# The beginning of a two-layer decoder kernel is rearranged: loads, splits, fillers, and the place of sums and maxima

## Chip, core and metric

One Trainium2 chip, one of its cores. The metric is the device time of one execution in microseconds (us); lower is better. Three runs of the kernel before gave 600.25, 600.36 and 603.13 us, with a median of 600.36 us.

## What is computed

Two layers over 256 tokens of width 1024, all in float32: an mLSTM mixer and a convolutional feed-forward, then block attention and a second feed-forward. Only the first steps of the mixer matter here:

```
u = rmsnorm(x, norm_g) @ w_in
q, k, v, o, gi, gf = split(u)            # 512, 512, 1024, 1024, 4, 4 columns
i_pre, f_pre = gi + b_gates[0], gf + b_gates[1]
lf   = log_sigmoid(f_pre);  bcum = cumsum(lf)          # over time
m_t  = running maximum over time of (i_pre - bcum)     # stabiliser
s    = (q k^T) * exp(decay built from bcum, i_pre, m_t)
h    = (s @ v) / max(|sum s|, exp(-m_t))
```

The norm needs one mean of squares per token; the kernel multiplies with unnormalised x (times the gain) and scales the products by that token's reciprocal root afterwards.

## The kernel before

Every float32 product is made from two parts. `split` (L176) and `unit` (L164) round an operand to a `hi` part on ScalarE (ACT) and leave the rest as `lo` on VectorE (DVE, `lo = raw - hi`); TensorE (PE) then runs hi times (hi, lo) as one 512-column matmul and lo times hi as one of 256 columns (`steps_w`, L227) or three of 512 columns (`steps_x`, L254). A weight unit is 128 x 2048 floats (1 MB): one DMA into one of three `raw` buffers, two halves on ACT, two on DVE into one of four `hi`/`lo` buffer pairs. A new load can go out only when DVE has read the buffer's last content, and a new `hi` can be made only when PE has finished with the buffer's last content.

PE's order is the order of the program (a manual schedule); `mix` (L69) runs a list of costed steps and calls other items when the running cost reaches the number written beside them. The orders of the other engines come from a scheduler when the kernel is built. So a place in PE's order is fixed by those numbers, and what stands ahead of an instruction on DVE or ACT must be read from the built program.

The beginning runs so. SP issues, in one queue, x (`hT`, 8 blocks of 128 rows), the gate weights and gains (`fst`), the first unit of `w_kq` in four pieces and the second in two, with the small broadcast `row` between those two (L103 to L117). PE runs eight warm-up matmuls (L129). x is split into `xa` by block (L181, L182). PE then runs eight steps k of three products each: the gates (L503) and the first two columns j = 0 and 1 of the eight k/q columns, five matmuls a step; then columns j = 2 to 7, eight steps of two matmuls each. Beside that:

- squares of x on GpSimd (POOL, L398), their running sum `sqacc` on DVE (L400);
- `r.sums` (L213) reads `sqacc` on PE, in column j = 2 after six of its steps; `ms` on DVE and `rc` on POOL (L217) follow;
- `gates` (L431) and `r.row` (L222) need `rc`; the columns j = 0 to 2 are read out of PSUM and scaled once `r.row` is there (L490), the others after that;
- `sums_f` (L444) and `maxima` (L453), late in the columns; `maxima` starts a chain of nine small DVE operations (L454, L458) that ends in `mh` (ACT) and `ml` (DVE) at L178 and L179;
- `tab` and `gcol` (L606 to L615), needed only in the second layer, on POOL.

Then come the v and o products (`block_x`, four blocks of two units of `w_vo`, sixteen steps of three 512-column matmuls). In the second of them stand the four `decay` items (L474, L475), which read `mh` and `ml`; after them `floors` and `scores`.

Of the kernel before, what the change touches and what calls it, by code (L numbers as in the profile page):

```python
# [18 lines left out]
P = 128  # L19
D = 1024  # L20
S = 256
# [18 lines left out]
WARM = 8  # L40
# [41 lines left out]
def yoco_kernel(ctx: ExitStack, tc: tile.TileContext, A, out):  # L82
# [41 lines left out]
    nc.scalar.activation(const.tile([P, 1], F32, name="tables"), mhalf[:, :1], AF.Exp)  # L124
    warm = const.tile([P, 512], BF16, name="warm")
    nc.vector.memset(warm, 0.0)
    for j in range(WARM):
        ps = pmis.tile([P, 512], F32, name="mis")
        nc.tensor.matmul(ps, warm[:, :P], warm, start=True, stop=True)  # L129
    nc.gpsimd.memset(wgs.bitcast(F32), 0.0)  # L130


    ident = const.tile([P, P], F32, name="ident")
    make_identity(nc, ident)

    both8 = const.tile([P, 2 * MH], F32, name="both8")
    nc.gpsimd.tensor_tensor(out=both8, in0=ident[:, :2 * MH], in1=ident[:, 2 * MH:4 * MH], op=OP.add)

    sel = const.tile([P, MH, P], F32, name="sel")
    nc.gpsimd.memset(sel, 0.0)  # L140
    nc.gpsimd.affine_select(out=sel, in_=sel, pattern=[[-1, MH], [0, P]],
                            compare_op=OP.not_equal, fill=1.0, base=0, channel_multiplier=1)

    tri = const.tile([P, S], F32, name="tri")
    nc.gpsimd.memset(tri, 1.0)
    nc.gpsimd.affine_select(out=tri[:, :P], in_=tri[:, :P], pattern=[[1, P]],
                            compare_op=OP.is_ge, fill=0.0, base=0, channel_multiplier=-1)

    cmask = const.tile([P, S], F32, name="cmask")
    nc.gpsimd.memset(cmask, 0.0)  # L150
    nc.gpsimd.affine_select(out=cmask[:, :P], in_=cmask[:, :P], pattern=[[1, P]],
# [649 lines left out]
```

## Time and profile before

| | |
|---|---|
| median of three runs | 600.36 us |
| profiled execution | 600.34 us, its span 598.6 us |
| PE busy / DVE / ACT / POOL | 590.3 / 494.1 / 392.7 / 172.3 us |
| PE first matmul of the gates, of the columns | 4.77 us, 7.36 us |
| PE at the sums (L213) | 20.90 us |
| PE at the first block of v and o | 37.80 us |
| PE at the first decay (L474) | 50.76 us |

Times count from the span's start. A matmul's row gives its own duration; since matmuls are pipelined, the pace is read from one start to the next.

### The profile page before, as it was taken

What the parts mean: (1) busy time and instruction counts of PE and PEld (TensorE: products, weight loads), DVE (VectorE), ACT (ScalarE), POOL (GpSimd) and SP (SyncE); (2) the same over time, 40 slices, a digit from 0 to 9 for tenths busy, and PEclk for the clock granted to TensorE, in tenths of its full rate; (3) what the DMA queues carried; (4) which work ended last, traced back from release to release, by engine and by line L of the source; (5) the groups of instructions that cost most, each with busy time, mean ns of one, the idle gap of its engine ahead of it and who ended that gap; (6) DMA issues with size and microseconds to landing.
All of it is one profiled execution on the core that took longest, in us unless ns stands there. A gap on an engine that the chain in (4) does not pass through costs nothing.

```text
span 598.6 us, 8993 instructions
## 1 busy us (share of the span) xinstructions
PE 590.3 (99%) x3278; PEld 506.2 (85%) x3278; DVE 494.1 (83%) x837; ACT 392.7 (66%) x713; POOL 172.3 (29%) x188
## 2 busy tenths in 40 slices
PE   7999999999999999999999999999999999999997
PEld 4888888888888888888888888888888888888887
DVE  5997678979999999987768687467999999998650
ACT  6656776577886767765656687554878767676430
POOL 6500300352545344301111210022546453432000
PEclk9999999999999999999999999999999999999999
DMA  7875334627445543486745533335363456336730
GB/s 249 305 275 178 141 140 142 211 79 273 153 172 175 206 156 115 166 263 215 240 183 211 194 123 125 126 140 209 123 225 146 165 187 211 105 138 208 266 111 19
DMA packets 18621, 105.79 MB, mean 177 GB/s; under 512 B 2320, under 2 KB 3856, under 8 KB 9104
## 3 DMA queue, kind: packets, MB, share of 16 engines
q1 hardware_dynamic: 18576, 105.21, 50.2%
q8 instruction: 26, 0.43, 0.3%
q14 instruction: 19, 0.16, 0.1%
HBM read 104.15 MB, written 1.05 MB: 176 GB/s over the span
## 4 chain that ended last, share of the span: by engine, by line
PE 87%; DVE 6%; ACT 3%; issue 1%; DMA 1%; POOL 1%; SPq 0%; DVEq 0%
PE acc L242 41%; PE acc L246 21%; PE acc L263 6%; PE acc L265 6%; PE acc L264 6%; DVE lo L173 3%; ACT hi L172 1%; DVE xs L349 1%; DVE xa L182 1%; DMA hT<-xT 1%; PE acc L240 1%; PE mis L554 1%; DVE hT L292 1%; PE mis L669 1%; PE acc L681 1%
## 5 line engine op out<-in xcount | busy, mean ns | idle before, releaser
L173 DVE TENSOR_TENSOR lo<-raw,hi 128x1024 fp32r<-128x1024 f32 (+2 forms) x218 | 248.5, 1169 | 29.4 <-ACT hi L172 29.3
L242 PE MATMUL acc<-xb,hi 128*128 128x512 f32 x736 | 252.3, 396 | 0.6 <-POOL xb L352 0.6
L172 ACT ACTIVATE hi<-raw 128x1024 fp32r<-128x1024 f32 (+2 forms) x218 | 199.8, 964 | 55.1 <-PE acc L242 28.8
L246 PE MATMUL acc<-xb,lo 128*128 128x256 f32 x736 | 191.2, 279 | 0.0
L242 PEld LDWEIGHTS acc<-xb,hi 128*128 128x128 f32 x736 | 131.8, 188 | 26.3 <-POOL xb L352 1.3
L246 PEld LDWEIGHTS acc<-xb,lo 128*128 128x128 f32 x736 | 138.7, 188 | 8.0
L242 PE MATMUL acc<-f,hi 128*128 128x512 f32 x330 | 115.0, 394 | 0.0
L330 DVE SCALAR_TENSOR_TENSOR y<-whole,par,y 128x254 f32<-128x254 f32 (+1 forms) x176 | 110.3, 646 | 3.1 <-ACT y L327 2.8
L246 PE MATMUL acc<-f,lo 128*128 128x256 f32 x352 | 96.8, 282 | 0.0
L339 POOL TENSOR_TENSOR a<-sg,y 128x256 f32<-128x256 f32 x44 | 58.7, 1334 | 97.6 <-ACT sg L337 97.6
L242 PEld LDWEIGHTS acc<-f,hi 128*128 128x128 f32 x330 | 61.1, 188 | 13.0
L246 PEld LDWEIGHTS acc<-f,lo 128*128 128x128 f32 x352 | 66.1, 188 | 1.3
L327 ACT ACTIVATE y<-whole,par 128x256 f32<-128x256 f32 x88 | 51.7, 595 | 20.8 <-DVE whole L283 18.8
L242 PE MATMUL acc<-xa,hi 128*128 128x512 f32 x160 | 58.3, 407 | 2.3 <-ACT hi L172 1.8
L263 PE MATMUL acc<-hi,xa 128*128 128x512 f32 x128 | 53.0, 414 | 0.0
L341 POOL TENSOR_TENSOR f<-a,f 128x256 fp32r<-128x256 f32 x44 | 42.3, 962 | 36.3 <-ACT f L340 36.3
L265 PE MATMUL acc<-hi,xa 128*128 128x512 f32 x128 | 50.1, 392 | 0.0
L264 PE MATMUL acc<-lo,xa 128*128 128x512 f32 x128 | 50.0, 391 | 0.0
L200 POOL TENSOR_TENSOR sqacc<-sqacc,sq 128x256 f32<-128x256 f32 x18 | 16.3, 907 | 115.3 <-ACT sq L199 115.3
L246 PE MATMUL acc<-xa,lo 128*128 128x256 f32 x160 | 44.8, 292 | 0.0
L282 ACT ACTIVATE whole<-acc 128x256 f32<-128x256 f32 x97 | 35.4, 368 | 7.7 <-PE acc L242 6.2
L283 DVE TENSOR_TENSOR whole<-acc,whole 128x256 f32<-128x256 f32 x97 | 39.4, 412 | 0.0
(183 smaller groups left out, 637.5 us busy)
## 6 DMA issues: line engine op xcount, KB each, us to landing
raw<-w_up SPq DMA_DIRECT2D x44, 1024.0 KB, 4.8
raw<-w_down SPq DMA_DIRECT2D x32, 704.0 KB, 4.3
raw<-w_kqv SPq DMA_DIRECT2D x12, 1024.0 KB, 4.8
raw<-w_vo SPq DMA_DIRECT2D x8, 1024.0 KB, 4.8
raw<-w_out SPq DMA_DIRECT2D x4, 1024.0 KB, 4.8
raw<-w_o SPq DMA_DIRECT2D x4, 1024.0 KB, 4.8
raw<-w_kq SPq DMA_DIRECT2D x2, 1024.0 KB, 7.6
raw<-w_kq SPq DMA_DIRECT2D x4, 256.0 KB, 5.7
```

Source lines behind the costliest of these rows:

```text
L172: nc.scalar.activation(hi[:, c], raw[:, c], AF.Copy)
L173: nc.vector.tensor_tensor(lo[:, c], raw[:, c], hi[:, c].bitcast(F32), OP.subtract)
L242: nc.tensor.matmul(p, hi[:, c], both[k], start=k == 0, stop=last)
L246: nc.tensor.matmul(p[:, :S], lo[:, c], xh[k], start=False, stop=False)
L263: nc.tensor.matmul(p, xh[k][:, ts], hi[:, c], start=k == 0, stop=False)
L264: nc.tensor.matmul(p, xh[k][:, ts], lo[:, c], start=False, stop=False)
L265: nc.tensor.matmul(p, xl[k][:, ts], hi[:, c], start=False, stop=k == KD - 1)
L283: nc.vector.tensor_tensor(y, ps[:, :S], y, OP.add)
L327: nc.scalar.activation(y, u, AF.Identity, bias=b, scale=w[2])
L330: nc.vector.scalar_tensor_tensor(y[:, d:], u[:, :S - d], w[j], y[:, d:], op0=OP.mult, op1=OP.add)
L339: nc.gpsimd.tensor_tensor(out=a, in0=sg, in1=y[0], op=OP.mult)
L341: nc.gpsimd.tensor_tensor(out=al[i], in0=a, in1=ah[i].bitcast(F32), op=OP.subtract)
```

## The change

It does seven things.

1. The loads of x go out on SP first; the first two pieces (256 KB each) of the first weight unit go out on ACT's queue, the other two on SP behind x; `row` is loaded behind the second unit.
2. The first two weight units are split by hand in a fixed order on ACT and DVE: block by block with x, in pieces of 256, 256, 512, 512, 512 and then 512, 512, 1024 columns, ahead of the squares.
3. The squares move from POOL to ACT (Square), their sums stay on DVE.
4. Ten warm-up matmuls instead of eight, and two fillers of the same kind behind the first step.
5. k and q columns are read out of PSUM into `kq` unscaled and are scaled in place at the end of the columns; no column's read-out waits for `r.row`.
6. `r.sums` moves from cost 1.5 to 6.6, `gates` and `r.row` from 3.2 to 9.5, and `sums_f` and `maxima` from the columns (9.6, 14.0) into the first block of v (1.5, 4.5). Within a step the gates' matmul comes last.
7. The constants are made behind all this in the program, the zeroing of `wgs` moves from POOL to DVE, and `gcol` and `tab` are kept where they stand in the program, behind the mixer.

```diff
-WARM = 8
+WARM = 10
+FILL = 2
...
     nc.sync.dma_start(hT[:, 0], A["xT"][:, 0])
     nc.sync.dma_start(fst, A["first"])
     nc.sync.dma_start(hT[:, 1], A["xT"][:, 1])
+    for j in range(3):
+        k = slice(2 * j + 2, 2 * j + 4)
+        nc.sync.dma_start(hT[:, k], A["xT"][:, k])
     for j in range(4):
         c = slice(j * 512, (j + 1) * 512)
-        nc.sync.dma_start(raw0[:, c], A["w_kq"][0, :, c])
-        if j < 3:
-            k = slice(2 * j + 2, 2 * j + 4)
-            nc.sync.dma_start(hT[:, k], A["xT"][:, k])
+        (nc.scalar if j < 2 else nc.sync).dma_start(raw0[:, c], A["w_kq"][0, :, c])
...
-        if j == 0:
-            nc.sync.dma_start(row, A["row"].to_broadcast([P, N_ROW]))
...
+    warm_up(WARM)
+    nc.vector.memset(wgs.bitcast(F32), 0.0)
...
+    first = ExitStack()
+    first.enter_context(tc.manual_schedule(engines={mybir.EngineType.Activation, mybir.EngineType.DVE}))
+    w0 = [wsp.tile([P, 2048], F32R, name=nm) for nm in ("hi", "lo")]
+    w1 = [wsp.tile([P, 2048], F32R, name=nm) for nm in ("hi", "lo")]
+
+    def piece(w, raw, a, b):
+        split(w[0][:, a:b], w[1][:, a:b], raw[:, a:b])
+
     for k in range(KD):
         split(setA[0][k], setA[1][k], hT[:, k], fst[:, C_ANORM + k:C_ANORM + k + 1])
+        if k < 2 or k % 2 == 1:
+            piece(w0, raw0, (k if k < 2 else k - 1) * 256, (k + 1) * 256)
+        if k == 0:
...
+    for a, b in ((0, 512), (512, 1024), (1024, 2048)):
+        piece(w1, raw1, a, b)
     for k in range(KD):
-        sq = work.tile([P, S], F32, name="sq") if k > 0 else sqacc
-        nc.gpsimd.tensor_tensor(out=sq, in0=hT[:, k], in1=hT[:, k], op=OP.mult)
-        if k > 0:
-            nc.vector.tensor_tensor(sqacc, sqacc, sq, OP.add)
+        squares(k, nc.vector)
+    first.close()
...
-        def kq_done(j):
-            nc.vector.tensor_tensor(kq[j], whole(pk[j]()), r.rB, OP.mult)
...
-                           (lambda p: kq_done(j)) if j > 2 else None)
+                           lambda p: whole(p, kq[j]))
+        def scale(j):
+            nc.vector.tensor_tensor(kq[j], kq[j], r.rB, OP.mult)
...
-        mix([s for k in range(KD) for s in (sg[k], s0[k], s1[k])])
+        for k in range(KD):
+            mix((s0[k], s1[k], sg[k]))
+            if k == 0:
+                warm_up(FILL)
         mix(kq_steps(2)[:1])
+        nc.sync.dma_start(row, A["row"].to_broadcast([P, N_ROW]))
         nc.sync.dma_start(par, A["par"])
         mix(kq_steps(2)[1:] + [s for j in range(3, 8) for s in kq_steps(j)],
-            [(1.5, r.sums), (3.2, gates), (3.2, row_done), (9.6, sums_f), (14.0, maxima)])
+            [(6.6, r.sums), (9.5, gates), (9.5, r.row)])
+        for j in range(2 * MH):
+            scale(j)
...
-        mix(block_x(A["w_vo"], 0, setA, v_done(0)))
+        mix(block_x(A["w_vo"], 0, setA, v_done(0)), [(1.5, sums_f), (4.5, maxima)])
...
-    nc.gpsimd.tensor_copy(gcol, par[:, C_KG:C_KG + 2])
+    tc.keep_in_program_order(nc.gpsimd.tensor_copy(gcol, par[:, C_KG:C_KG + 2]))
```

Where a DVE or ACT instruction lands in the built program is seen in the two orders. First DVE, around the last additions into the sum of squares. Names end in a buffer's number: `raw_94` is the second unit of `w_kq`, `raw_375` or `raw_360` the third, `raw_431` or `raw_428` the fourth, `raw_502` the first unit of `w_vo`, and `ms` is the instruction behind PE's sums. Before, from the second unit's last half on:

```order
L173 TENSOR_TENSOR lo_298<-raw_94,hi_297 128x1024
L283 TENSOR_TENSOR whole_290<-acc_214,whole_290 128x256
L283 TENSOR_TENSOR whole_351<-acc_253,whole_351 128x256
L400 TENSOR_TENSOR sqacc_167<-sqacc_167,sq_202 128x256
L283 TENSOR_TENSOR whole_355<-acc_256,whole_355 128x256
L400 TENSOR_TENSOR sqacc_167<-sqacc_167,sq_205 128x256
L173 TENSOR_TENSOR lo_378<-raw_375,hi_377 128x1024
L215 TENSOR_SCALAR ms_320<-mis_317 128x2
```

In the changed kernel, the last twelve rows up to `ms`; ahead of them stand the same half of the second unit, three additions and three read-outs:

```order
L172 TENSOR_TENSOR sqacc_141<-sqacc_141,sq_189 128x256
L145 TENSOR_TENSOR lo_363<-raw_360,hi_362 128x1024 x2
L172 TENSOR_TENSOR sqacc_141<-sqacc_141,sq_192 128x256
L256 TENSOR_TENSOR kq2_261<-acc_320,kq2_261 128x256
L172 TENSOR_TENSOR sqacc_141<-sqacc_141,sq_195 128x256
L145 TENSOR_TENSOR lo_431<-raw_428,hi_430 128x1024 x2
L256 TENSOR_TENSOR kq3_262<-acc_341,kq3_262 128x256
L172 TENSOR_TENSOR sqacc_141<-sqacc_141,sq_198 128x256
L145 TENSOR_TENSOR lo_505<-raw_502,hi_504 128x1024
L172 TENSOR_TENSOR sqacc_141<-sqacc_141,sq_201 128x256
L145 TENSOR_TENSOR lo_505<-raw_502,hi_504 128x1024
L187 TENSOR_SCALAR ms_384<-mis_381 128x2
```

So the last addition, which PE's sums wait for, now stands behind both halves of the third and of the fourth unit and the first half of the fifth.

Second DVE again, around `ml`, which the second matmul of each decay reads (`V11` is the last v read-out of the first block; `raw_757` and `raw_764` are the sixth unit of `w_vo`, whose `hi` needs the buffer that the first block's last step frees). Before:

```order
L173 TENSOR_TENSOR lo_712<-raw_709,hi_711 128x1024 x2
L179 TENSOR_TENSOR ml_225<-mx0_220,mh_224 4x256
L540 SCALAR_TENSOR_TENSOR V11_506<-acc_558,rc_322,V10_505 128x2x256
L173 TENSOR_TENSOR lo_760<-raw_757,hi_759 128x1024
L477 SCALAR_TENSOR_TENSOR E0_230<-mis_604,av_218,cmask_137 128x256
```

In the changed kernel:

```order
L475 TENSOR_TENSOR mx0_246<-mx1_247 4x256
L559 SCALAR_TENSOR_TENSOR V11_493<-acc_565,rc_386,V10_492 128x2x256
L145 TENSOR_TENSOR lo_767<-raw_764,hi_766 128x1024 x2
L151 TENSOR_TENSOR ml_251<-mx0_246,mh_250 4x256
L494 SCALAR_TENSOR_TENSOR E0_255<-mis_611,av_244,cmask_220 128x256
```

`ml` has moved behind the read-out and behind both halves of the sixth unit. On ACT the same holds of `mh`, which the first matmul of each decay reads. Before:

```order
L172 ACTIVATE hi_711<-raw_709 128x1024 x2
L178 ACTIVATE mh_224<-mx0_220 4x256
L539 ACTIVATE V10_505<-acc_558,rc_322 128x2x256
L172 ACTIVATE hi_759<-raw_757 128x1024 x2
L481 ACT_TABLE_LOAD
```

In the changed kernel:

```order
L144 ACTIVATE hi_718<-raw_716 128x1024 x2
L558 ACTIVATE V10_492<-acc_565,rc_386 128x2x256
L144 ACTIVATE hi_766<-raw_764 128x1024 x2
L150 ACTIVATE mh_250<-mx0_246 4x256
L498 ACT_TABLE_LOAD
```

There `mh` stands behind both halves of that unit's `hi`.

## Rows read from the trace of the kernel before

**Rows 1.** The page: engines (busy, share, instructions) and the chain that ended last.

```profile
PE 590.3 (99%) x3278; PEld 506.2 (85%) x3278; DVE 494.1 (83%) x837; ACT 392.7 (66%) x713; POOL 172.3 (29%) x188
...
PE 87%; DVE 6%; ACT 3%; issue 1%; DMA 1%; POOL 1%; SPq 0%; DVEq 0%
```

**Rows 2.** Timeline of PE: start, duration, line, operation; in brackets idle time and its releaser.

```profile
7.36 0.79 PE L242 MATMUL acc<-xa,hi 128*128 128x512 f32 x1 [1.83 <-ACT hi L172]
...
9.11 0.63 PE L503 MATMUL acc<-xa,hi 128*128 128x512 f32 x1
...
10.81 0.63 PE L503 MATMUL acc<-xa,hi 128*128 128x512 f32 x1
...
14.05 0.40 PE L503 MATMUL acc<-xa,hi 128*128 128x512 f32 x1
...
14.99 0.40 PE L503 MATMUL acc<-xa,hi 128*128 128x512 f32 x1
...
18.26 0.40 PE L242 MATMUL acc<-xa,hi 128*128 128x512 f32 x1
...
18.61 0.39 PE L242 MATMUL acc<-xa,hi 128*128 128x512 f32 x1
...
20.90 0.58 PE L213 MATMUL mis<-tri,sqacc 128*128 128x1 f32 x4 [0.83 <-DVE sqacc L400]
```

**Rows 3.** Timeline of ACT: the second unit's last half, same columns.

```profile
14.82 1.06 ACT L172 ACTIVATE hi<-raw 128x1024 fp32r<-128x1024 f32 x1 [1.25 <-DMA raw<-w_kq]
```

**Rows 4.** Windows: busy us and instructions by engine, clock, DMA share, GB/s.

```profile
4.50:6.50 2.00, 1.03 (x2) 0.29 (x1) 0.70 (x2) 0.51 (x1) 2.00 (x5) 1.00 0.73 127
...
7.50:11.00 3.50, 3.50 (x10) 2.67 (x11) 2.97 (x6) 3.02 (x7) 1.94 (x6) 1.00 1.05 406
11.00:13.00 2.00, 2.00 (x8) 1.61 (x7) 2.00 (x5) 2.00 (x5) 0.79 (x1) 1.00 0.57 220
```

**Rows 5.** Timeline of SP: issues of the first load and of weight pieces.

```profile
0.81 0.38 SPq L103 DMA_DIRECT2D hT<-xT  x1
...
2.18 0.43 SPq L108 DMA_DIRECT2D raw<-w_kq  x1
```

**Rows 6.** DMA issues within 2.2 to 2.4 us: count, size, us from issue to landing.

```profile
raw<-w_kq SPq DMA_DIRECT2D x1, 256.0 KB, 4.5
```

**Rows 7.** Timeline of DVE: two halves of one unit, then read-outs and scalings.

```profile
34.80 2.34 DVE L173 TENSOR_TENSOR lo<-raw,hi 128x1024 fp32r<-128x1024 f32 x2
37.07 0.41 DVE L490 TENSOR_TENSOR kq<-whole,rB 128x256 f32<-128x256 f32 x1
37.41 0.41 DVE L283 TENSOR_TENSOR whole<-acc,whole 128x256 f32<-128x256 f32 x1
```

**Rows 8.** Groups by line and form, DVE, 3 to 60 us: count, busy us, mean ns.

```profile
L182 DVE SCALAR_TENSOR_TENSOR xa<-hT,fst,xa 128x256 fp32r<-128x256 f32 x8 | 4.2, 530 | 1.2 <-ACT xa L181 1.1
```

**Rows 9.** Timelines of PE, ACT and DVE around the first decay.

```profile
50.76 0.28 PE L474 MATMUL mis<-mh,selr 128*128 128x256 f32 x1
50.87 0.28 PE L475 MATMUL mis<-ml,selr 128*128 128x256 f32 x1
...
48.11 0.40 ACT L178 ACTIVATE mh<-mx 4x256 fp32r<-4x256 f32 x1
...
49.51 2.00 ACT L172 ACTIVATE hi<-raw 128x1024 fp32r<-128x1024 f32 x2
...
49.57 0.41 DVE L179 TENSOR_TENSOR ml<-mx,mh 4x256 fp32r<-4x256 f32 x1
```

**Rows 10.** POOL: groups within 16 to 24 us, then its timeline and PE's near 120 us.

```profile
L614 POOL TENSOR_TENSOR tab<-rope,row 128x32 f32<-128x32 f32 x4 | 3.1, 786 | 0.0
...
117.16 0.74 POOL L200 TENSOR_TENSOR sqacc<-sqacc,sq 128x256 f32<-128x256 f32 x1 [3.14 <-ACT sq L199]
121.04 0.71 POOL L217 TENSOR_TENSOR rc<-ms,mhalf 128x2 f32<-128x2 f32 x1 [3.15 <-DVE ms L215]
...
122.47 0.38 PE L222 MATMUL mis<-ident,rc 128*128 128x128 f32 x2
```

More of the change, by code (lines that the diff above doesn't have):

```diff
@@ L122, in yoco_kernel @@
     nc.gpsimd.memset(mhalf, -0.5)
-    nc.scalar.activation(const.tile([P, 1], F32, name="tables"), mhalf[:, :1], AF.Exp)
     warm = const.tile([P, 512], BF16, name="warm")
     nc.vector.memset(warm, 0.0)
[L127 to L136, printed above, removed]
@@ L160, in yoco_kernel, with warm_up @@
-    amask = const.tile([P, S], BF16, name="amask")
-    nc.gpsimd.tensor_copy(amask, amaskf)
-    def unit(src, length, raw=None, pieces=PIECES):
-        if raw is None:
-            raw = wraw.tile([P, 2048], F32, name="raw")[:, :length]
-            nc.sync.dma_start(raw, src)
+    nc.scalar.activation(const.tile([P, 1], F32, name="tables"), mhalf[:, :1], AF.Exp)
+    def warm_up(n):
+        for j in range(n):
+            ps = pmis.tile([P, 512], F32, name="mis")
+            nc.tensor.matmul(ps, warm[:, :P], warm, start=True, stop=True)
@@ L168, in unit @@
+    warm_up(WARM)
+    nc.vector.memset(wgs.bitcast(F32), 0.0)
+    def unit(src, length, pieces=PIECES):
+        raw = wraw.tile([P, 2048], F32, name="raw")[:, :length]
+        nc.sync.dma_start(raw, src)
         hi = wsp.tile([P, 2048], F32R, name="hi")[:, :length]
@@ L277, in acc, with whole @@
         return pacc.tile([P, 512], F32, name="acc")
-    def whole(ps):
-        y = work.tile([P, S], F32, name="whole", bufs=WHOLE)
+    def whole(ps, y=None):
+        if y is None:
+            y = work.tile([P, S], F32, name="whole", bufs=WHOLE)
         nc.scalar.activation(y, ps[:, S:], AF.Copy)
@@ L387, in pair_k @@
         return pair(i, [k])
-    wgv = wgs.rearrange("p (k m) -> p k m", k=KD)
-    split(wgv[:, :, :2 * MH], wgv[:, :, 2 * MH:4 * MH],
-          fst[:, :KD * 2 * MH].rearrange("p (k m) -> p k m", k=KD))
+    first = ExitStack()
[4 more added lines that the diff above has]
+        split(w[0][:, a:b], w[1][:, a:b], raw[:, a:b])
@@ new lines, in yoco_kernel @@
+    tri = const.tile([P, S], F32, name="tri")
+    nc.gpsimd.memset(tri, 1.0)
+    nc.gpsimd.affine_select(out=tri[:, :P], in_=tri[:, :P], pattern=[[1, P]],
+                            compare_op=OP.is_ge, fill=0.0, base=0, channel_multiplier=-1)
+    cmask = const.tile([P, S], F32, name="cmask")
+    nc.gpsimd.memset(cmask, 0.0)
+    nc.gpsimd.affine_select(out=cmask[:, :P], in_=cmask[:, :P], pattern=[[1, P]],
+                            compare_op=OP.is_ge, fill=BIG, base=0, channel_multiplier=-1)
@@ L403, in yoco_kernel @@
+    identb = const.tile([P, P], BF16, name="identb")
+    nc.gpsimd.tensor_copy(identb, ident)
+    amaskf = const.tile([P, S], F32, name="amaskf")
+    nc.gpsimd.memset(amaskf, 0.0)
+    nc.gpsimd.affine_select(out=amaskf[:, P:], in_=amaskf[:, P:], pattern=[[-1, P]],
+                            compare_op=OP.is_ge, fill=-BIG, base=0, channel_multiplier=1)
+    amask = const.tile([P, S], BF16, name="amask")
+    nc.gpsimd.tensor_copy(amask, amaskf)
     with tc.tile_pool(name="mls", bufs=1, reuse_waits="tile") as mp, \
@@ L484, in yoco_kernel @@
         kq = [mp.tile([P, S], F32, name=f"kq{j}") for j in range(2 * MH)]
-        wk = [Once(lambda u=u: unit(A["w_kq"][u], 2048, *((raw0, 4), (raw1, 2), (), ())[u])) for u in range(4)]
+        wk = [Once(lambda u=u: unit(A["w_kq"][u], 2048)) for u in range(4)]
+        wk[0].made, wk[1].made = w0, w1
         pk = [Once(acc) for j in range(2 * MH)]
-        def kq_done(j):
-            nc.vector.tensor_tensor(kq[j], whole(pk[j]()), r.rB, OP.mult)
         def kq_steps(j):
             return steps_w(pk[j], wk[j // 2], lambda k: k * 256 + (j % 2) * P, setA, range(KD), KD,
-                           (lambda p: kq_done(j)) if j > 2 else None)
-        def row_done():
-            r.row()
-            for j in range(3):
-                kq_done(j)
+                           lambda p: whole(p, kq[j]))
+        def scale(j):
+            nc.vector.tensor_tensor(kq[j], kq[j], r.rB, OP.mult)
         def gate_step(k):
```

41 lines of the change are left out of this document (17 added, 24 removed).

## Prediction

> **What bounds the kernel now.** The page comes first: PE is busy 590.3 of 598.6 us and the chain that ended last is PE's for 87% [rows 1]. So a microsecond counts only if PE gets ahead of it or stops for it, and the question for each edit is when PE passes a fixed place in its order. Next comes the timeline of PE in the first 21 us [rows 2]. Each of the eight first steps, five matmuls, ends with the gates' one (L503): from 9.11 to 10.81 us one step takes 1.70 us, from 14.05 to 14.99 us it takes 0.94. That is TensorE's lower and upper level (1.2 and 2.4 GHz), although the granted clock in the windows reads 1.00 throughout [rows 4]; between 10.81 and 14.05 us it rose, and PE had been at work without a break since 7.36. A step of a later column takes 0.35 us (18.26 to 18.61). At 20.90 PE had waited 0.83 us for the sum of squares. Then the windows of the loads [rows 4]: 127 GB/s from 4.5 to 6.5 us, 406 from 7.5 to 11 us, 220 from 11 to 13 us, where the small broadcast `row` lands. Last the places where DVE and ACT hand something to PE: the second unit's last half [rows 3], and `mh` and `ml` before the first decay [rows 9].
>
> The sum is made against the profiled execution (600.34 us, span 598.6 us and 1.74 us around it), which lies 0.02 us under the median of 600.36 us.
>
> **The place from which I count.** Between the sums (20.90 us) and the first decay (50.76 us) PE takes 29.86 us [rows 2, 9]. In the changed kernel the sums stand 16 column steps further on (after six steps of j = 4 instead of j = 2); `gates`, `r.row`, `sums_f` and `maxima` still lie between the two places. So from the sums to the first decay it has 29.86 - 16 x 0.35 = 24.26 us of PE's work left. What remains is when PE can do its sums, and what stops it at the decay.
>
> **Term 1: when the sums can run.** They wait for the last addition on DVE. By the new order DVE must do, from the second unit's last half on: six halves of units (one of the second, two each of the third and fourth, the first of the fifth), seven additions and five read-outs. Two halves take 2.27 us (34.80 to 37.07), so 1.14 us each; a 256-column operation follows the next after 0.34 us [rows 7]. That makes 6 x 1.14 + 12 x 0.34 = 10.9 us, behind ACT's 1.06 us on that last half [rows 3]: 12.0 us after the half has landed. Before, only one of those halves stood ahead of the last addition.
>
> When does it land? Before, at 14.82 us [rows 3]. `row` is now behind it. In the 2 us in which `row` landed the loads ran at 220 instead of 406 GB/s [rows 4], worth 2 x (1 - 220/406) = 0.9 us: 13.9 us. ACT's queue lets the first weight piece go out at 0.81 us, like SP's first load, instead of 2.18 [rows 5], so at most another 1.37 us, and at the least nothing: the stream was slow in 4.5 to 6.5 us with its engines busy 0.73 of the time [rows 4], so requests were not what it lacked. I take the middle, 0.7 us: 13.2 us, with ends 12.5 and 13.9.
>
> "Issuing engines are not separate DMA queues" in the Trainium skill's page "DMA: Bandwidth & Descriptors" says that loads issued by two engines run on the same 16 DMA engines and interleave, and that a second issuer saves only the time to issue. By that the sum would take 13.9 us and come to 602.4 us, where my middle gives 601.7; the share of 0.73 speaks for the page.
>
> DVE gives a floor as well. Before that half it has eight `xa` (4.2 us by [rows 8]) and weight pieces of together 3072 columns, as many as three halves: 3.4 us. It can start when the first weight piece is there, at 0.81 + 4.5 = 5.3 us with the duration that this piece had before [rows 6]. 5.3 + 4.2 + 3.4 + 10.9 = 23.8 us, under 13.2 + 12.0 = 25.2 us. So the sums run at **25.2 us**, with 24.5 (landing at 12.5) and 25.9 as ends.
>
> PE itself would be there sooner. Its first step can start near 6 us, eight steps take between 8 x 0.94 and 8 x 1.70 us, two fillers 0.5 to 0.9 us, and the 22 column steps 7.7 us: 21.7 us at the upper level throughout, 27.8 at the lower throughout. With the rise no later behind its first step than before, near 12.5 us, six us at the lower level hold some 3.5 of the eight steps, and PE arrives near 24.5 us. So the ten warm-ups, the fillers and the earlier clock cost or bring nothing: the wait for DVE covers them up to 25.2 us. The earlier weight pieces are in the landing already.
>
> Without more, PE is at the first decay at 25.2 + 24.26 = 49.5 us instead of 50.76: **-1.3 us**.
>
> **Term 2: the first decay.** It reads `mh` (ACT) and `ml` (DVE). Before, `mh` was made at 48.11 and `ml` at 49.57, ahead of their need at 50.76 and 50.87 us [rows 9]. Now both stand behind the sixth unit of v, whose halves ACT cannot start before the first block's end. In the times of before that is 49.51 us, and ACT is through at 51.51 us [rows 9]; `mh` with its 0.40 us is there at 51.9. DVE follows the second half (ready at 51.5) with 1.14 us, then `ml` with 0.41 us: 53.2 us. PE wants `ml` at 50.87. **+2.4 us**, and this wait moves with PE, however early it comes, since the block's end starts it. The chain of maxima, nine operations of 0.34 us from the block's middle on, stands ahead of all this and is no later.
>
> **Term 3: the tables on POOL.** `tab` and `gcol` leave the beginning, where they covered nothing that PE waits for, and now run behind POOL's last addition near 117.9 us. Four of the six pieces took 786 ns each in the beginning [rows 10], so all six up to 4.7 us. The next `rc` stood at 121.04 with 0.71 us, and PE read it at 122.47. Behind 4.7 us it is ready at 123.3, 0.8 us late; at half that length, without a neighbour's load, it is in time. I take **+0.3 us**.
>
> **Edits at nothing.** Squares on ACT: they run beside DVE's longer queue; without that cover the last would be eight of some 0.34 us, 2.7 us. `wgs` on DVE: a fill of 1024 columns in the 5.3 us before DVE's first piece; uncovered it would be about the 1.14 us of as many columns. Scaling in place: eight operations of 0.34 us as before, needed only at the scores. `row` is needed at the gates, behind the sums, and is there by then.
>
> **Sum.** -1.3 + 2.4 + 0.3 = +1.4 us: 600.34 + 1.4 = **601.7 us**. With a landing at 12.5 us and no late `rc` it is 600.7; at 13.9 and 0.8 it is 602.9.
>
> **The rivals.** Half a per cent, about what a measurement of this kernel tells from no change, is 3.0 us.
>
> *Slower: the second unit lands no earlier.* Each microsecond on its landing is one on the end, since DVE's 12.0 us behind it are fixed. The change in total is the landing minus 11.8 us (12.0 + 24.26 - 50.76 + 2.7). At 14.8 us, the time of before, it is +3.0 us; at 15.8 it is +4.0 (604.3 us). Two queues in turn could do that by letting the first weight pieces take turns with `fst` and x, so that DVE's first pieces start late too. For it: the slow windows up to 6.5 us. Against: `row` is out of the way. It decides from 14.8 us on.
>
> *Faster: neither new wait ends last.* If DVE were through with the additions by 21.7 us and `mh` and `ml` early enough, PE would reach the decay at 46.0 us: -4.8 us, 595.5 us. For it: PE has the whole front at the upper level. Against: landing would have to be at 9.7 us, and the built order puts both behind the sixth unit.
>
> *Middle: the second queue brings nothing.* Only `row`'s 0.9 us is gained, the landing is 13.9 us and the end 602.4 us, inside the same band. The page named above would have it so.
>
> *Only one wait.* If the decay's wait were absorbed, 601.7 - 2.4 = 599.3 us; also inside the band.
>
> **How the numbers follow.** The forecast with its ends, 600.7 to 602.9, has 0.36; the second queue without effect 0.20; one wait only 0.08: together 0.64 within 3.0 us of 600.34. The slower rival has 0.23, the faster one 0.13, for it asks two things that the order speaks against. The range leaves out most of the faster case and the far end of the slower: 597.8 to 604.2.
>
> **What would show it.** Right: PE's sums wait 2 to 3.5 us for DVE's addition near 25 us; the second unit's last half starts on ACT at 12.5 to 14 us; the first decay waits about 1.1 us for `mh` and 1.3 more for `ml`; first block of v near 36 us; PE at the upper level before 12 us. Wrong: no wait at the decay, sums before 23 us, or that half landing after 14.8 us.

## The result, and the profile after

The changed kernel takes **604.59 us** (median of 11 executions, 602.20 to 606.98); the kernel before, beside it, 601.44 us (median of 11, 600.16 to 603.13). The ratio is 1.006, with a 95% interval of 1.0041 to 1.0078: slower by 0.6%. The forecast of 601.7 us with "no change" was wrong, and the time lies 0.4 us above the range.

The executions are not alike. The profiler gives each its mean granted clock. The three at 1.000 took 602.20 to 602.30 us, the three at 0.997 took 603.98 to 604.59, the two at 0.994 took 605.70 and 605.97, the three at 0.992 took 606.65 to 606.98. The time goes up with each step of the mean clock, by 1.0 to 2.1 us, and the lowest group is the forecast within 0.6 us. The profiled execution has 0.994: 605.70 us, span 603.9.

The page's engines and chain, beside [rows 1]: PE is 2.1 us busier in a span that is 5.3 us longer.

```profile
PE 592.4 (98%) x3282; PEld 506.8 (84%) x3282; DVE 494.1 (82%) x840; ACT 395.2 (65%) x723; POOL 164.9 (27%) x179
...
PE 86%; DVE 7%; DMA 2%; ACT 2%; POOL 1%; issue 1%; SPq 0%; POOLq 0%; DVEq 0%
```

The timeline of PE (start, duration, line, operation, in brackets the wait), beside [rows 2, 9]. L516 is the gates' product of a step, L185 the sums, L491 and L492 the decay's `mh` and `ml`, L484 the floors.

```profile
5.93 0.77 PE L214 MATMUL acc<-xa,hi 128*128 128x512 f32 x1 [0.23 <-DVE xa L154]
...
7.09 0.39 PE L516 MATMUL acc<-xa,hi 128*128 128x512 f32 x1
...
14.91 0.40 PE L516 MATMUL acc<-xa,hi 128*128 128x512 f32 x1
...
25.94 0.58 PE L185 MATMUL mis<-tri,sqacc 128*128 128x1 f32 x4 [2.95 <-DVE sqacc L172]
...
26.81 0.28 PE L218 MATMUL acc<-xa,lo 128*128 128x256 f32 x1
...
28.61 0.63 PE L214 MATMUL acc<-xa,hi 128*128 128x512 f32 x1
...
29.25 0.63 PE L214 MATMUL acc<-xa,hi 128*128 128x512 f32 x1
...
30.80 0.28 PE L218 MATMUL acc<-xa,lo 128*128 128x256 f32 x1
...
51.34 0.39 PE L237 MATMUL acc<-hi,xa 128*128 128x512 f32 x1
52.66 0.38 PE L491 MATMUL mis<-mh,selr 128*128 128x256 f32 x1 [0.93 <-ACT mh L150]
54.44 0.57 PE L492 MATMUL mis<-ml,selr 128*128 128x256 f32 x1 [1.39 <-DVE ml L151]
...
56.09 0.41 PE L491 MATMUL mis<-mh,selr 128*128 128x256 f32 x1
...
57.79 0.33 PE L491 MATMUL mis<-mh,selr 128*128 128x256 f32 x1
...
59.72 0.38 PE L484 MATMUL mis<-ident,mx 128*128 128x128 f32 x2
```

Read it from the top. The front is quicker than forecast: the upper level is there in the first step, the gates' last step stands at 14.91 us, and PE stands ready for the sums at 22.99 us. Then it stops for 2.95 us. **Behind the stop a column step takes 0.64 us (28.61 to 29.25) instead of 0.35**: the clock has fallen to its lower level (1.2 GHz), until 30.5 us. The same at the decay: two stops of 0.93 and 1.39 us, and then the decays come 1.7 us apart (56.09 to 57.79). In the timeline of the kernel before, whose first decay is at 50.76 us, they were 0.92 apart; its floors (L467) are the second row:

```profile
51.68 0.28 PE L474 MATMUL mis<-mh,selr 128*128 128x256 f32 x1
...
54.48 0.38 PE L467 MATMUL mis<-ident,mx 128*128 128x128 f32 x2
```

The windows (start and end, length; busy us and instructions of PE, PEld, DVE, ACT and POOL; then the granted clock, the DMA share and GB/s) show it in the third figure from the end:

```profile
25.00:30.00 5.00, 4.06 (x18) 3.62 (x19) 4.60 (x7) 2.91 (x4) 2.75 (x1) 0.72 0.90 311
27.00:27.50 0.50, 0.50 (x3) 0.41 (x2) 0.50 (x1) 0.34 (x2) 0.42 (x1) 0.68 1.24 524
27.50:30.50 3.00, 3.00 (x11) 2.56 (x10) 2.10 (x3) 0.76 (x2) 2.33 (x1) 0.50 0.87 292
30.50:31.00 0.50, 0.50 (x5) 0.46 (x4) 0.00 (x0) 0.00 (x0) 0.00 (x0) 0.91 1.05 410
...
50.00:60.00 10.00, 7.67 (x31) 5.96 (x30) 7.35 (x14) 5.46 (x8) 0.00 (x0) 0.83 0.57 210
54.50:55.00 0.50, 0.50 (x2) 0.50 (x3) 0.00 (x0) 0.00 (x0) 0.00 (x0) 0.50 0.56 229
55.00:57.50 2.50, 2.50 (x9) 2.02 (x8) 1.49 (x4) 0.52 (x1) 0.00 (x0) 0.50 0.90 298
57.50:58.00 0.50, 0.50 (x4) 0.40 (x3) 0.00 (x0) 0.47 (x1) 0.00 (x0) 0.60 1.08 459
```

So the granted clock is at half from about 27.2 to 30.6 us and from about 54.5 to 57.9 us, 3.4 us each time. Half the clock for 3.4 of 604 us lowers the mean by 0.003. So the means 0.997, 0.994 and 0.992 are those of one, two and three such lengths; where they lay is known for the profiled execution alone.

The timelines of ACT and DVE at the two stops, beside [rows 3, 9]: the second unit's last half is the last 1.06 us of the first row, so it starts at 13.28 us; the last addition is done at 25.79, and `ml` at 54.39.

```profile
12.04 2.30 ACT L150 ACTIVATE hi<-raw 128x512 fp32r<-128x512 f32 x3 [0.23 <-DMA raw<-w_kq]
...
52.21 0.40 ACT L150 ACTIVATE mh<-mx 4x256 fp32r<-4x256 f32 x1
...
18.02 2.36 DVE L145 TENSOR_TENSOR lo<-raw,hi 128x1024 fp32r<-128x1024 f32 x2 [0.42 <-ACT hi L144]
...
25.37 0.42 DVE L172 TENSOR_TENSOR sqacc<-sqacc,sq 128x256 f32<-128x256 f32 x1
...
53.98 0.41 DVE L151 TENSOR_TENSOR ml<-mx,mh 4x256 fp32r<-4x256 f32 x1
```

How far the changed kernel is behind at places that both pass, with the kernel before's times:

| place in PE's order | before | after | behind |
|---|---|---|---|
| sums (before: 20.90 + 16 steps of 0.35) | 26.50 | 25.94 | -0.56 |
| `ml` of the first decay | 50.87 | 54.44 | +3.57 |
| floors | 54.48 | 59.72 | +5.24 |
| last matmul | 594.92 | 600.20 | +5.28 |

Everything has happened by the floors. Of the 4.13 us between the first two places, 2.76 are the decay's stops: without them `mh` would follow the matmul at 51.34 after 0.23 us, and `ml` would follow `mh` after 0.11, but they come 1.09 and 1.67 us later than that. (The 0.93 and 1.39 us in brackets count from the end of the matmul ahead, and in a row the next one starts before that end.) The lower level behind the sums is 1.5 us: seven column steps from 26.81 to 30.80 take 3.99 us, where 7 x 0.35 is 2.45. The gates and `r.row` take some 0.2 us less than before. The 1.67 us to the floors are the lower level again. Without these 3.2 us of slow clock this execution would have been at 602.5 us; the executions at full clock are at 602.2 to 602.3.

### The profile page after: what moved, and what is told of

It reads as the page before. It is cut to its first block, busy times and chain, and to the rows that moved or that the text cites. A ratio compares the mean times of both kernels' runs of the same rounds, so it can differ in the third digit from the quotient of the medians.

```text
span 603.9 us, 8996 instructions
## 1 busy us (share of the span) xinstructions
PE 592.4 (98%) x3282; PEld 506.8 (84%) x3282; DVE 494.1 (82%) x840; ACT 395.2 (65%) x723; POOL 164.9 (27%) x179
## 4 chain that ended last, share of the span: by engine, by line
PE 86%; DVE 7%; DMA 2%; ACT 2%; POOL 1%; issue 1%; SPq 0%; POOLq 0%; DVEq 0%
PE acc L214 41%; PE acc L218 21%; PE acc L235 6%; PE acc L237 6%; PE acc L236 6%; DVE lo L145 4%; DMA raw<-w_kq 1%; POOL xb L325 1%; ACT hi L144 1%; PE acc L212 1%; DMA hT<-xT 1%; DVE xa L154 1%; PE mis L573 1%; DVE hT L265 1%; PE mis L689 1%
## 5 line engine op out<-in xcount | busy, mean ns | idle before, releaser
L145 DVE TENSOR_TENSOR lo<-raw,hi 128x1024 fp32r<-128x1024 f32 (+1 forms) x212 | 241.8, 1171 | 26.0 <-ACT hi L144 25.8
L144 ACT ACTIVATE hi<-raw 128x1024 fp32r<-128x1024 f32 (+1 forms) x212 | 195.3, 969 | 53.6 <-PE acc L214 27.8
L313 ACT ACTIVATE f<-a 128x256 fp32r<-128x256 f32 x44 | 18.2, 413 | 28.7 <-POOL a L312 28.6
L214 PEld LDWEIGHTS acc<-xa,hi 128*128 128x128 f32 x160 | 30.3, 193 | 7.9 <-issue 1.1
```

Of the source, the lines that this page charges most:

```text
L144: nc.scalar.activation(hi[:, c], raw[:, c], AF.Copy)
L145: nc.vector.tensor_tensor(lo[:, c], raw[:, c], hi[:, c].bitcast(F32), OP.subtract)
L214: nc.tensor.matmul(p, hi[:, c], both[k], start=k == 0, stop=last)
L313: nc.scalar.activation(ah[i], a, AF.Copy)
```

## Experiments

The theory to test: the change makes two stops, each costs its own length and, in most executions, a fall of the clock behind it. The rivals: the stops alone; DVE late whatever is moved; the loads; the fillers. Unless another kernel is named, an edit is one to the changed kernel, and a median stands beside that of the kernel before on the same chip: 600.2 us beside the runs e1 to e8, 600.3 beside e9 and e12, 601.4 beside e13 and e14. The changed kernel's 604.59 us stands beside 601.44. In every group the executions of the kernel before lie either at 600.0 to 600.8 us or at 601.3 and more, and its median moves with the share of the second kind. So a difference between medians of two groups is good to about a microsecond, and executions of the same mean clock compare better.

### The sums later (e1_sums_later)

```diff
-            [(6.6, r.sums), (9.5, gates), (9.5, r.row)])
+            [(10.6, r.sums), (13.0, gates), (13.0, r.row)])
```

> The changed kernel with the sums moved 12 column steps further on (and gates and r.row with them), so that PE has some 4.2 us more of its own work before it wants DVE's last addition. Theory (two new waits of PE, 2.95 us at the sums and 2.32 us at the first decay, and behind either one the clock falls to the lower level in most executions, costing about 1.7 us each time): the wait at the sums is gone and with it the stretch at the lower level from 27 to 30 us; the decay's wait stays. 602.25 us (the changed kernel's executions at a mean clock of 1.000) less 2.95 = 599.3 us where the clock holds at the decay too, 601.0 where it falls there: median 599.3 to 601.3. Rival A (the waits cost only their own length, the clock nothing): 604.6 - 2.95 = 601.6 us. Rival B (DVE is behind anyway, so that the time comes back as a longer wait at the gates or the decay): 604 us or more.

605.23 us (604.08 to 608.13). The stop at the sums is gone and another has come, at `sums_f`, in the list of PE's waits (us in total, times, longest):

```profile
PE mis L461 <- DVE lf L457: 3.2, 1, 3.2
PE mis L492 <- DVE ml L151: 1.4, 1, 1.4
...
PE mis L491 <- ACT mh L150: 0.9, 1, 0.9
```

Rival B holds here: `gates` comes later too and `sums_f` does not, and DVE does seven scalings, a read-out and two halves between the two steps of `lf` (35.20 and 40.22 us). Putting off PE's question also put off the chain that hangs on its answer.

### The decay later (e2_decay_later)

```diff
-            at(1.8, 0.6, decay, [(h,) for h in range(MH)]) + [(4.2, floors)]
-            + at(5.1, 1.2, scores, [(h,) for h in range(MH)]))
+            at(4.4, 0.5, decay, [(h,) for h in range(MH)]) + [(6.6, floors)]
+            + at(7.2, 0.9, scores, [(h,) for h in range(MH)]))
```

> The changed kernel with the first decay moved four steps of v further on (cost 1.8 to 4.4; floors and scores behind it, closer together). Theory: the 2.32 us of waiting for mh and ml are covered, so 602.25 - 2.3 = 600.0 us where the clock holds behind the sums, 601.7 where it falls there: median 600.0 to 602.0. Rival A (waits only): 604.6 - 2.3 = 602.3 us. Rival B (the stop only moves to the scores or to the heads of the next block, which now have less room): 603.5 us or more, with a wait of PE at L540 or in the heads.

602.09 us (599.58 to 603.48), 2.5 less than the changed kernel, and no new stop. By mean clock: 599.58 and 599.60 us at 1.000, five executions at 0.997 with 601.21 to 602.09, five at 0.994 with 602.70 to 603.48. At full clock that is 2.7 us under the changed kernel's 602.25, what its decay's stops cost by the starts in the table above (2.76), and more than the 2.3 expected. The sums' stop (2.6 us in the profile) still brings the lower level: ten of twelve executions have it in their mean, and in the profiled one (602.70 us) it lasts twice as long as in the changed kernel's, with a granted clock of 0.50 from 26 to 32 us.

### Both (e3_both_later)

> Both moves together. Theory: neither wait and no fall of the clock before 100 us, 602.25 - 2.95 - 2.32 = 597.0 us, faster than both kernels; every execution at a mean clock of 0.999 or more. Rival A (waits only, clock nothing): 604.6 - 5.3 = 599.3 us. Rival B (DVE behind anyway): 602 us or more, with the wait at the gates, at the decay or at the scores.

602.08 us (599.78 to 603.93): no better than the decay alone. The theory's 597.0 us fell, since the stop for `lf` of the first run is here too, 2.7 us, and the clock falls behind it (0.87 in 40 to 50 us).

### Fillers in the stops (e4_fillers_in_waits)

```diff
-            [(6.6, r.sums), (9.5, gates), (9.5, r.row)])
+            [(6.6, lambda: (warm_up(13), r.sums())), (9.5, gates), (9.5, r.row)])
...
-            at(1.8, 0.6, decay, [(h,) for h in range(MH)]) + [(4.2, floors)]
+            [(1.8, lambda: warm_up(10))] + at(1.8, 0.6, decay, [(h,) for h in range(MH)]) + [(4.2, floors)]
```

> The changed kernel with its two places left where they are, and matmuls of zeros put into the waits: 13 of 512 columns (0.227 us each at the upper level, 2.95 us) ahead of the sums and 10 (2.27 us) ahead of the first decay. They do nothing but keep PE at work. Theory: the sums still run near 25.9 us and the decay near 54 less what the clock had cost, the granted clock stays at 1.00 behind both, and the time is that of the executions at full clock, 602.3 us, with little spread. Rival A (the clock's fall costs nothing, or is not brought about by the pause): 604.6 us, and the same spread of clocks. Were the fillers in the way they would cost at the most a few tenths.

603.22 us (602.12 to 603.74), and all five executions at a mean clock of 0.999 or 1.000. PE's timeline has the fillers, and the two windows that stood at 0.72 and 0.83 are at 1.00:

```profile
23.65 2.98 PE L131 MATMUL mis<-warm 128*128 128x512 bf16 x13
27.09 0.58 PE L185 MATMUL mis<-tri,sqacc 128*128 128x1 f32 x4 [0.45 <-DVE sqacc L172]
```

```profile
25.00:30.00 5.00, 4.55 (x26) 3.23 (x25) 3.85 (x7) 3.10 (x4) 0.71 (x1) 1.00 0.86 303
50.00:60.00 10.00, 9.58 (x48) 6.91 (x47) 7.51 (x16) 6.38 (x11) 0.00 (x0) 1.00 0.59 210
```

Matmuls of zeros, which compute nothing and bring no operand earlier, take the means of 0.997 and less out of the spread: none of five, where the changed kernel had eight of eleven. That is the theory's point. The median is 1.4 us lower, but across two groups. It is 0.9 us over the 602.3 us that the theory named: in the profiled execution (603.74 us) PE's first step starts at 6.37 us and DVE's last addition comes 1.15 us later than in the changed kernel's profile. So part of it is the front of that execution; of the others there is no trace.

### A stop put into the kernel before (e8_before_sums_earlier)

```diff
-            [(1.5, r.sums), (3.2, gates), (3.2, row_done), (9.6, sums_f), (14.0, maxima)])
+            [(0.0, r.sums), (3.2, gates), (3.2, row_done), (9.6, sums_f), (14.0, maxima)])
```

> The kernel before, with the sums five column steps earlier (cost 1.5 to 0): PE gets there near 18.6 us and stops for DVE's last addition, which stays where it was (20.90 us), so that the wait grows from 0.83 us to some 2.4. The steps it would have done follow behind: +1.6 us by the wait alone, 601.8 us. Theory (a pause of this length lets the clock fall): the granted clock behind it is under 1.00 in most executions and the time 601.8 + 1.7 = 603.5 us in those; median 602.5 to 603.7. Rival (the clock falls in the changed kernel for another cause, as its denser front): 601.8 us, the clock not lower than in the kernel before. The order on DVE and ACT behind the sums also shifts a little; a new wait there would show by itself in the list of waits.

604.61 us (603.50 to 604.75), all at 0.992 or 0.994. The timeline of PE, beside the last row of [rows 2]:

```profile
20.83 0.74 PE L213 MATMUL mis<-tri,sqacc 128*128 128x1 f32 x4 [3.85 <-DVE sqacc L400]
...
22.43 0.63 PE L242 MATMUL acc<-xa,hi 128*128 128x512 f32 x1
...
23.07 0.63 PE L242 MATMUL acc<-xa,hi 128*128 128x512 f32 x1
```

The sums run when they ran before (20.83 against 20.90 us), PE has stopped 3.85 us instead of 0.83 (2.4 were expected; PE was there at 16.98, not near 18.6), and steps of 0.64 us follow up to 24.4 us; the granted clock of 20 to 25 us is 0.66 instead of 1.00. The mean of 0.994 counts a second low stretch, in the front (granted clock 0.57 from 7 to 11 us), so the window shows the fall and not the mean. The profiled execution (603.50 us) adds up: five steps behind the sums instead of ahead, 1.75 us, and five steps at the lower level, 5 x 0.29 = 1.5 us, are 3.2 on 600.3. So the fall needs nothing of the changed front; a stop is enough. The other four executions are 0.7 to 1.3 us longer; why stays open.

### One queue (e6_one_queue)

```diff
-        (nc.scalar if j < 2 else nc.sync).dma_start(raw0[:, c], A["w_kq"][0, :, c])
+        nc.sync.dma_start(raw0[:, c], A["w_kq"][0, :, c])
```

> The changed kernel with the first two pieces of the first unit back on SP's queue, behind x: all loads on one queue, row still behind the second unit. My term for the second queue was 0.7 us on the landing of the second unit's last half, between 0 and 1.37: the half would land near 14.0 us instead of 13.3, the sums run at 26.6, the time be 605.3 us (604.6 + 0.7). By the rival that the second queue brings nothing: landing 13.3 us, 604.6 us. Since the first weight piece is then asked for behind x, near 4.5 us instead of 0.8, PE's first step starts later, near 9 instead of 6 us; that costs nothing as long as PE is at the sums before DVE: the wait there is shorter by what PE is later, and the clock has less of a pause to fall in, which could take back up to 1.7 us (602.9 to 605.3 together).

608.30 us (607.24 to 609.36), 3.7 us more than the changed kernel and outside of what I allowed. The first piece is asked for at 3.59 us instead of 0.79, ACT has it at 9.45 us instead of 4.92, and the sums run at 29.08 us:

```profile
9.45 0.42 ACT L150 ACTIVATE hi<-raw 128x256 fp32r<-128x256 f32 x1 [5.51 <-DMA raw<-w_kq]
...
29.08 0.58 PE L185 MATMUL mis<-tri,sqacc 128*128 128x1 f32 x4 [0.90 <-DVE sqacc L172]
```

DVE cannot start its chain without the first piece, and from 9.90 us on it hardly stops until the last addition. So the early first piece is worth 3.1 us at the sums, through DVE's whole queue, not 0.7 us through the landing of the second unit. That unit's last half lands 1.0 us later, about as expected (issued at 6.43 us and there after 7.8, against 6.07 and 7.2), but ACT comes to it only at 15.62 us and does not wait for it. The run takes the place in the queue away together with the queue; that the queue as such, rather than the early place, gives this is not shown.

### Without fillers and with eight warm-ups (e7_no_fillers)

```diff
-WARM = 10
-FILL = 2
+WARM = 8
+FILL = 0
```

> The changed kernel with 8 warm-up matmuls instead of 10 and no fillers behind the first step. I put both at nothing. Theory: PE rises to the upper level later or not, but comes to the sums before DVE's last addition at 25.9 us either way (at the lower level throughout not before 27.8); the time is 604.6 us, or less by up to 1.7 where PE comes so late that the pause is too short for the clock to fall; the decay's wait and fall stay. Rival (the fillers and the earlier clock are what makes the front quick): PE passes the sums after 27 us, 605.7 us or more.

605.15 us (602.63 to 605.88). In the profile PE stops 2.07 us for its first operand, and the granted clock is 0.57 from 7 to 11 us and 0.91 over the first 20 us; the gates' last step stands at 15.66 us instead of 14.91, and the sums run at 26.05 us instead of 25.94, after a stop of 2.3 us. As argued: the front has slack against DVE, and the fillers are worth nothing that can be told here.

### The additions on POOL, the decay later (e5_pool_adds)

```diff
-        squares(k, nc.vector)
+        squares(k, nc.gpsimd, spare[k])
```

`spare` holds seven tiles that are free at that time (the four of `E`, three of `kq`), where two buffers took turns. The edit also takes the squares out of the order fixed by hand on ACT.

> The changed kernel with the decay moved as in the run before (e2_decay_later), and the seven additions of the squares on POOL, which does nothing there from 10 us on, out of free tiles instead of two buffers; DVE then does the halves of the units without them in between. Theory: the sums no longer wait for DVE; POOL has the last square near 11 us and is through 7 x 0.8 us later, at some 17 to 20 us, before PE comes at 23. The additions' 7 x 0.34 us also leave DVE's queue, so that gs, lf and the rest come no later. No wait over 1 us before 100 us, clock 1.00 throughout: 599.6 (e2 at full clock) - 2.95 = 596.7 us, every run at 0.999 or more, faster than both kernels. Rival A (DVE is behind anyway): the stop returns at gates, at lf for sums_f or at the decay, 599.5 us or more. Rival B (the squares in ACT's queue hold up its halves of the weights): first steps of PE late, the gates' last step after 15.5 us, 598 us or more.

599.78 us (599.59 to 600.80); ratio 0.9991 (0.9982 to 0.9999). All eleven executions are at 0.999 or 1.000 and no stop over 1 us stands behind the first step: that half of the theory holds. The time does not. Rival B: the squares now run between ACT's first halves, and POOL's additions slow DVE beside them; the gates' last step comes at 17.58 us instead of 14.91. What each of the two costs is not told apart. Timelines of DVE and POOL: a pair of `xa` takes 1.51 and 1.84 us, beside 0.87 for a pair in the changed kernel.

```profile
10.02 1.51 DVE L154 SCALAR_TENSOR_TENSOR xa<-hT,fst,xa 128x256 fp32r<-128x256 f32 x2 [0.25 <-ACT xa L153]
...
12.78 1.84 DVE L154 SCALAR_TENSOR_TENSOR xa<-hT,fst,xa 128x256 fp32r<-128x256 f32 x2
...
9.43 2.71 POOL L173 TENSOR_TENSOR sqacc<-sqacc,E 128x256 f32<-128x256 f32 x3 [0.94 <-ACT E L172]
12.22 3.01 POOL L173 TENSOR_TENSOR sqacc<-sqacc,kq 128x256 f32<-128x256 f32 x3
```

### The additions ahead on DVE (e9_squares_spare, e12_squares_spare_only)

```diff
-    for k in range(KD):
-        squares(k, nc.vector)
-    first.close()
...
+        spare = [sqacc] + [e[:, :S] for e in E] + kq[:4:-1]
+        for k in range(KD):
+            squares(k, nc.vector, spare[k])
+        first.close()
```

With two buffers for the squares ACT could be only two ahead of DVE's additions, and the built order filled the time with halves of the third and fourth units. With seven there is one such half between the additions, as DVE's timeline of the first run shows. The first run also has the decay later, the second not.

> The changed kernel with the decay moved as in e2_decay_later, and the squares written to seven tiles that are free at that time instead of two buffers in turn. ACT then makes all eight in a row behind the second unit, and DVE can add them up ahead of the halves of the third and fourth unit, in the time in which it waited for the third unit to land (0.4 to 0.8 us at 18 us in the changed kernel). The additions stay on DVE, so that POOL is out of it (in e5_pool_adds DVE's xa took 0.9 us each beside POOL's additions instead of 0.44). Theory: last addition near 20 us, PE passes the sums without a stop at 23 us, no wait over 1 us before 100 us, clock at 1.00: 599.6 (e2 at full clock) - 2.95 = 596.7 us, every run at 0.999 or more, faster than both kernels by 0.6%. Rival A (DVE is behind with the halves anyway, the sums' wait only showed it first): the wait comes back at a low half of the third or fourth unit, at the gates or at lf for sums_f, 599 us or more, with the clock down behind it in some runs. Rival B (eight squares in a row hold up ACT's evictions of the first columns): PE waits for a free accumulator near 17 to 20 us, 598 us.

598.48 us (597.31 to 600.02); ratio 0.9963 (0.9949 to 0.9977): faster than both. PE passes the sums without a stop, at 24.20 us in an execution whose first steps were at the lower level. Behind the first step one stop is left up to 100 us, for POOL's `rc`. Timelines of DVE, PE and POOL:

```profile
20.65 1.22 DVE L145 TENSOR_TENSOR lo<-raw,hi 128x1024 fp32r<-128x1024 f32 x1
21.78 0.42 DVE L173 TENSOR_TENSOR sqacc<-sqacc,kq 128x256 f32<-128x256 f32 x1
...
29.23 0.43 PE L195 MATMUL mis<-ident,rc 128*128 128x128 f32 x2 [0.93 <-POOL rc L190]
...
26.43 2.75 POOL L190 TENSOR_TENSOR rc<-ms,mhalf 128x2 f32<-128x2 f32 x1 [20.48 <-DVE ms L188]
```

> The same squares in spare tiles, but the first decay where the changed kernel has it. Theory (waits add up, and each is followed by its own fall of the clock): 596.7 + 2.3 for the decay's wait = 599.0 us where the clock holds, 600.7 where it falls behind the decay: median 599.0 to 601.0, as far above the run before as e2_decay_later was below the changed kernel (604.6 - 602.1 = 2.5 us). Rival (the two are not independent: earlier by 3 us, PE finds mh and ml still later, since the chain of maxima on DVE does not come earlier with it): the decay's wait grows from 2.3 to 4 us or more and the time is 602 us or more.

602.12 us (600.92 to 603.23), 1.1 over the upper end. At a mean clock of 1.000 it takes 600.92 to 602.07 us, over the 599.0 expected there, so not all of the 1.1 is the clock; where the rest lies is not shown. The decay's stops are 0.93 and 1.39 us to the hundredth, although PE comes to them 4 us earlier (48.45 instead of 52.66): the stop moves with PE, as the prediction said, and the rival's longer one is not there. Decay moved or not makes 3.6 us between the medians of these two runs: the stops, and with them the lower level, which the profile has from 50 to 60 us (granted clock 0.68) and seven of the twelve executions in their mean.

### `r.row` later, and more warm-ups (e13_row_later, e14_row_later_warm12)

```diff
-            [(6.6, r.sums), (9.5, gates), (9.5, r.row)])
+            [(6.6, r.sums), (9.5, gates), (11.0, r.row)])
```

This is an edit to the kernel of e9; the second run has `WARM = 12` as well.

> e9_squares_spare with r.row five column steps later (9.5 to 11.0). There PE stopped 0.93 us for POOL's rc, which took 2.75 us beside two halves of DVE instead of the 0.71 us it takes alone. Theory: that stop is covered by 1.7 us of column steps, nothing behind it is later but the scalings on DVE, which are wanted at the scores only: 598.5 - 0.9 = 597.6 us. Rival: the later scalings push lf or the halves of the fourth unit back on DVE and PE stops there: 598.5 us or more.

597.78 us (596.78 to 598.56); ratio 0.9949 (0.9935 to 0.9964), all six executions at 1.000. In its profile (596.78 us) the sums stand at 22.90 us, 3.04 earlier than in the changed kernel, and behind its first step PE's longest stop up to 140 us is 0.3 us:

```profile
22.90 0.50 PE L186 MATMUL mis<-tri,sqacc 128*128 128x1 f32 x4
...
28.67 0.38 PE L195 MATMUL mis<-ident,rc 128*128 128x128 f32 x2
```

> The same with 12 warm-up matmuls instead of 10. In the profile of e9_squares_spare the warm-ups end at 5.7 us, PE waits 0.71 us for its first operand and then does its first 14 matmuls at the lower level, up to 10.4 us; in that of e12_squares_spare_only they run at the upper level after a wait of 0.84 us, and the gates' last step is 1.35 us earlier (14.81 against 16.16). Theory: with the gap filled PE goes into its first step at the upper level every time: 597.0 us with less spread than without. Rival (the level there hangs on something else, or two more warm-ups stand in the way of an early first piece): the same as or 0.3 us over the run beside it.

597.63 us (596.78 to 598.50); ratio 0.9947 (0.9933 to 0.9961): the same as with ten, and the spread no smaller. Its profile has a gates' last step at 15.05 us, no earlier. The rival holds.

## Why the prediction was wrong

**The order of DVE and ACT: right.** Both new stops were read from it, at their places: 2.95 us at the sums near 25.9 us (2 to 3.5 near 25 forecast), and 0.93 and 1.39 us at the decay (1.1 and 1.3 forecast, 2.32 in total against 2.4). That the decay's stop starts with the block's end, however early PE comes, was shown by e12. Two figures given beforehand were off, which changes nothing here. Up to `ms` the changed order has seven additions, as the prediction counts: two, not three, stand ahead of the rows shown (15.51 and 16.51 us). And the terms given for `ml` (51.5, 1.14 and 0.41) make 53.1 us and a wait of 2.2, not 53.2 and 2.4.

**What failed is the step that set the clock at nothing.** It stands in term 1: "the ten warm-ups, the fillers and the earlier clock cost or bring nothing", with the clock looked at only as something that rises. The sum then priced the two stops by their length alone and has no term for a fall behind them. In the trace both stops are followed by a stretch at the lower level, 1.5 us lost behind the sums and 1.7 behind the decay; 8 of 11 executions have one to three lengths of it in their mean clock. Fillers in the stops took it away (e4), and a longer stop in the kernel before brought it (e8). With the clock up throughout the changed kernel takes 602.25 us, 0.55 above the forecast and inside its ends: the sums 0.7 us and the decay's stops 0.4 us over their terms, the tables 0.3 and the gates 0.2 us under. Of the 2.3 us from there to 604.59, an execution with a mean of 0.997, one low stretch is some 1.6; the rest, 0.7 us, stays open. The row that could have warned was in hand: the two levels, and that PE had "been at work without a break" before it rose [rows 2].

**Term 1, the sums: 0.7 us too early.** 25.94 us against 25.2, 0.04 above the upper end (24.5 to 25.9). The landing was right: the half starts on ACT at 13.28 us, 13.2 forecast. The last addition is done 12.5 us behind it, not 12.0: DVE was taken to work without a gap, and it waited 0.42 us for ACT's half of the third unit. The front of PE was better than thought: there at 22.99 us, not near 24.5, which only made the stop longer. (The 27.8 us "at the lower throughout" leaves the 22 column steps at their upper-level price; at 0.64 us each it would be some 34. No measured time came near either.)

**The second queue: the landing about right, the worth not.** I gave it 0.7 us on the landing of the second unit. By e6 the early request for the first piece is worth 3.1 us at the sums, through the point at which DVE can begin, which I had used only as a floor (23.8 us) and not compared with the case without it. The floor was also closer than thought: DVE was through with the pieces ahead of that half at 14.00 us, and the half of ACT that it then waited for came 0.37 us later. "Issuing engines are not separate DMA queues" in the Trainium skill's page "DMA: Bandwidth & Descriptors" says that a second issuer saves the time to issue. The trace agrees with that in kind, 0.79 us against 3.59 for the first piece, but here that time stands at the head of a chain.

**Term 3: nothing, not 0.3 us.** POOL's tables took 3.2 us (123.05 to 126.25) and not 4.7, and the next `rc` at 126.37 with 0.71 us is there before PE reads it at 127.78, without a wait. Timelines of POOL and PE:

```profile
125.79 0.46 POOL L633 TENSOR_TENSOR tab<-rope,row 128x32 f32<-128x32 f32 x2
126.37 0.71 POOL L189 TENSOR_TENSOR rc<-ms,mhalf 128x2 f32<-128x2 f32 x1
...
127.78 0.38 PE L194 MATMUL mis<-ident,rc 128*128 128x128 f32 x2
```

**Fillers, squares on ACT, scaling in place: nothing, as said**, the first by e7, the others by their absence from PE's waits. But the two buffers that the squares take in turn set where the additions stand in DVE's order, and so the stop at the sums (e9).

**The slower rival** got the direction but not the cause: the second unit did land earlier (13.28 us, not 14.8), and the time came from elsewhere.

## What to carry to other kernels

Where the matrix engine is busy all the time, a stop in it can cost more than its length: here stops of 2.3 to 3 us were in most executions followed by a slower stretch that cost another 1.6 us, or twice that where it lasted twice as long. When a step is moved against a chain on another engine, work out when that chain ends and give PE other work up to there; if there is none, matmuls of zeros keep the clock. And before a consumer is moved later, see what lies behind its answer: the better repair was to let the short additions pass the long halves on DVE, by giving them buffers of their own, which with the decay and `r.row` moved gave 597.8 us, 0.5% under the kernel before beside it (601.4 us; 0.4% under the 600.2 to 600.3 of the other groups).

## What the runs showed that was not expected

- The clock falls in some executions and not in others behind the same stop. With a stop at the sums of 2.95 us (this kernel) and 2.6 us (e2) in the profiled executions, 3 of 11 and 2 of 12 have a mean of 1.000; how long their own stops were is not known.
- Among the profiled executions the stops sort cleanly. Taking those that PE made after it had been at the upper level: behind each of nine single stops of 1.9 to 4.6 us a low stretch follows, and behind each of the five pairs of 0.93 and 1.39 us at the decay. Behind single stops of 0.4 to 1.4 us, three of 0.67 to 0.96 us within 7 us in e5, none does. No run varies the length alone.
- A mean clock under 1.000 has a price only where PE has work there: the kernel before took 600.0 to 600.5 us in most of its executions at 0.997, as at 1.000, and over 601.3 us in all but one of those at 0.993 or 0.994.
- POOL's `rc`, 128 x 2 elements, takes 0.70 us in the kernel before, 1.62 in e5, where DVE had one half of a unit in hand (26.16 to 27.38 us), and 2.75 in the changed kernel, e9 and e13, where it had two; in each of these four it ends 0.6 us after the last half in hand. With DVE's `xa` twice as long beside POOL's additions in e5, the two engines hinder each other. The Trainium skill's page "GPSIMD Engine Reference", section "Key points", says that POOL shares its SBUF interfaces with VectorE and that an instruction of DVE with two inputs from SBUF contends; these rows agree.
